# A hybrid attention and RWKV-7 layer on one core: triangular inverse issued behind the rates, unmasked and whole-run copies, projections cut into parts between the chain's links, two accumulator banks swapped

## The chip, the cores and the metric

The kernel runs on one core of one Trainium2 chip, as one launch. The metric is the time of an execution on the device in microseconds (us), lower is better. The time before is the median of three runs.

## The reference, cut to what matters

One decoder layer on x of shape (1, 512, 1024) in float32: a half-step SwiGLU network (FFN1), a mixing stage, and a second half-step SwiGLU network (FFN2). The change lies in the mixing stage alone. There one projection gives seven pieces of 512 columns; three feed a dilated attention of 8 heads, four an RWKV-7 recurrence of 8 heads of size 64.

```
proj = rms_norm(x) @ W_in                       # 1024 -> 7 x 512
q, k, v, rr, rk, rv, rc = split(proj)
att = dilated_attention(qknorm(q), qknorm(k), v)
r, k, v = lerp(rr, mu_r), lerp(rk, mu_k), lerp(rv, mu_v)   # o[t] = x[t] + (x[t-1] - x[t]) * mu
decay, a, g = small networks of rc
kk = k * k_k / norm per head
k = k * (1 + (a - 1) * k_a)
# per head, over 512 tokens:
#   S_t = S_{t-1} diag(decay_t) + (S_{t-1} (-kk_t)) (kk_t a_t)^T + v_t k_t^T ;  y_t = S_t r_t
out = (groupnorm(y) + sum(r * k * r_k) * v) * g            # the second term is called bonus here
x = x + concat(att, out) @ W_out
```

## The kernel before, in words

**Matmuls.** Large products are made from three matmuls of 128x128 by 128x512: high part by high part (line 73), low part by high part (76), high part by low part (77). A weight comes in as `raw_...` by a DMA that SyncE issues; ScalarE (ACT) rounds it to `hi_...` (line 68), VectorE (DVE) makes `lo_... = raw - hi` (line 69). One projection of 128 output columns, `proj(j, ct)`, is 24 such matmuls into a bank `in{j}_{ct}`; j is the piece (0 to 2 for q, k, v, 3 to 5 for r, k, v of the recurrence, 6 for c), ct = 0..3 the block of 128 columns, which is two heads.

**The recurrence in chunks.** The 512 tokens are cut into 8 chunks of 64. `keys1(ct)` and `keys2(ct)` prepare a block of two heads: the lerp of k, a scan of the log decays (`cs`, DVE), two exponentials (`pb`, `pi`, ACT), the normalised key. The per-head factor `hrkk` is a power on GpSimd (POOL); `spread` copies it out to 128x512 (`rbkk`, `rbk`, line 463) for four transposes on TensorE (PE). At the end of `keys2` 32 small matmuls per block write `ab{ct}{h}`, the 64x64 matrices of each chunk and head. Of each, two diagonal 32x32 quarters go into `nst` (line 547), multiplied by the mask `smask`, and one off-diagonal quarter into `nof` (line 550).

**The inverse.** `invert` inverts the 128 triangular 32x32 blocks at once: `nst` is transposed into `au`, then 31 steps, each of a product `pr` (line 582) and a subtraction into `tu` (line 584) on DVE, each pair needing the pair before it. Two transposes write `ud` and `td` (lines 588, 589). POOL copies quarters of them into `tm` and `um`. `whole(ct)` copies the diagonal blocks from `ud` into `tbd`, the matrix of whole inverses (line 608), and makes the off-diagonal ones by matmuls on PE (`w`, `u`, each with copies behind it). Only the entries of `nst` below the diagonal enter these steps.

**Rates and chain.** `rates(ct)` makes the lerps of v and r (projections 5 and 3), `rt`, and the bonus (`bo`, `bv`), whose multiplication of r is line 563. Then comes the chain of 16 links gi = 0..3 (two pairs of blocks by two halves of the sequence) by c = 0..3, one after the other, each link four heads at one chunk: PE `cx` (line 806) from the state `sv`, a DVE copy `xc`, PE `cs` with `tbd`, copies into `sv`, PE `cn` (line 823), two DVE adds into the next state (line 827), two DVE adds into `ysb` (line 829). Around the links lie `pre(gi)` (products `aa` and others), `post(gi)` (norm and gate of the output, its transposes `yo` at line 856), `qkv(ct)` (projections 0 to 2 of the attention) and the attention of (gi, c, h), in stages. A list of events `ev`, sorted by a time written out by hand, sets in which order these are issued.

**Order on the engines.** Each engine runs its instructions in a fixed order. A scheduler sets it when the kernel is built, by priorities that follow the order of the code; work under `tc.high_priority()` goes ahead of what is issued before it. A buffer is given out again when its last reader is done. The chain has two accumulator banks, "ch" (`px`, name `cx`, and `pn`, name `cn`) and "y" (`pa`, name `cs`).

```
    with tc.high_priority():
        inv = invert()
    for ct in range(NCT):
        rates(ct)
        if ct:
            whole(ct - 1, *inv)
    whole(NCT - 1, *inv)
```

Of the kernel before, what the change touches and what calls it, by code (L numbers as in the profile page):

```python
# [19 lines left out]
P = 128  # L20
# [308 lines left out]
def mixing(mc, tc, I, xT, hook, weights, mm3, proj_into, vecs, ident, nhalf, new_xT, npool, spool, dpool, set_tp, ps_c, ps_y, begin):  # L329
# [8 lines left out]
    def pm(shape, name):  # L338
        return ps_m.tile(shape, F32, tag="mm", name=name)
# [4 lines left out]
    def pc(shape, name):  # L344
        return ps_c.tile(shape, F32, tag="ch", name=name)
# [31 lines left out]
    def proj(j, ct):  # L377
        acc = pm([P, S], f"in{j}_{ct}")
        proj_into([acc], [weights(I['w_in'][j * 4 + ct], P, f"in{j}_{ct}", lo_eng=G if j == 4 else None)], xT)
        return acc  # L380


    accs = [pm([P, S], f"in6_{ct}") for ct in range(2)]
# [76 lines left out]
    def spread(r, tmp, name):  # L460

        rb = tmp([P, 8, CH], f"rb{name}")
        V.tensor_copy(out=rb, in_=r.unsqueeze(2).broadcast_to([P, 8, CH]))
        ps = pt([P, S], f"sp{name}")
        rv = rb.rearrange("p (a b) c -> p a (b c)", b=2)
        for tt in range(NT):
            T.transpose(out=ps[:, tt * P:(tt + 1) * P], in_=rv[:, tt, :], identity=ident)
        return ps
# [7 lines left out]
    def ch(t_):  # L476
        return t_.rearrange("p (c t) -> p c t", t=CH)
# [44 lines left out]
    def keys2(ct):  # L522
# [17 lines left out]
        for h in range(2):  # L540
            p_ = half(h)
            ps = pt([P, NCH, CH], f"ab{ct}{h}")
            for c in range(NCH):
                T.matmul(ps[p_, c, :], ch(bt)[p_, c, :], ch(at)[p_, c, :], start=True, stop=True)
            for b in range(2):
                q_, t_ = slice(64 * h + 32 * b, 64 * h + 32 * b + 32), slice(32 * b, 32 * b + 32)
                V.tensor_tensor(out=nstv[q_, 8 * ct:8 * ct + 8, :], in0=ps[q_, :, t_],
                                in1=smask[q_, t_].unsqueeze(1).broadcast_to([32, NCH, 32]), op=ALU.mult)
            for e in range(2):
                A.copy(out=noff[quad(h, e), :, quad(h, 1 - e)], in_=ps[quad(h, 0), e::2, 32:64])  # L550
# [22 lines left out]
    def invert():  # L573
# [13 lines left out]
        td = npool.tile([P, 32, 32], F32, tag="gain", bufs=1, name="td")  # L587
        V.transpose(out=ud.rearrange("p a b -> p (a b)"), in_=tu.rearrange("p a b -> p (a b)"))
        V.transpose(out=td.rearrange("p a b -> p (a b)"), in_=tu.rearrange("p t j -> p j t"))

        uv, tv = (z.rearrange("p t (c m e) -> p c m e t", m=4, e=2) for z in (ud, td))
        um, tm = (tmp([P, NCT, 4, 32], n) for n in ("um", "tm"))
        for h in range(2):
            for e in range(2):
                G.tensor_copy(out=tm[quad(h, e)], in_=tv[quad(h, 0), :, :, e])
                G.tensor_copy(out=um[quad(h, 1 - e)], in_=uv[quad(h, 1), :, :, e])
        return ud.rearrange("p t (a j b c) -> p a b j c t", a=2, j=2, b=2), um, tm

# [3 lines left out]
    def whole(ct, udv, um, tm):  # L602

        cp, j = ct // 2, ct % 2
        for hf in range(2):
            for q in range(4):
                q_ = slice(32 * q, 32 * q + 32)
                (V.tensor_copy if q % 2 else A.copy)(out=tbd[q_, 2 * cp + hf, j, :, q_], in_=udv[q_, cp, hf, j])
        w = tmp([P, 4, P], f"w{ct}")
# [17 lines left out]
    def qkv(ct):  # L627
        tq = lambda shape, name: gp.tile(shape, F32, tag="tq", bufs=2, name=name)
        at = lambda shape, n, t=F32R: gp.tile(shape, t, tag=f"at{n}", bufs=2, name=f"{n}{ct}")
        acc = proj(0, ct)  # L630
        sq = tq([P, S], f"sqq{ct}")
# [8 lines left out]
        G.tensor_scalar(out=nq, in0=rq, scalar1=-1.0, scalar2=0.0, op0=ALU.mult, op1=ALU.add)  # L640
        acc = proj(1, ct)
        sq = tq([P, S], f"sqk{ct}")
# [3 lines left out]
        hr = head_scale(sq, 1.0 / 64, EPS, ALU.mult, ALU.add, f"k{ct}")  # L646
        acc = proj(2, ct)
        v0 = tq([P, S], f"v0{ct}")
# [9 lines left out]
        for h in range(2):  # L658
            A.copy(out=kh[half(h), h, :], in_=kT[half(h)])
            Q.dma_start(out=kh[half(1 - h), h, :].bitcast(F32), in_=kh[half(h), h, :].bitcast(F32))  # L660
            G.tensor_tensor(out=kl[half(h), h, :], in0=kT[half(h)], in1=kh[half(h), h, :].bitcast(F32), op=ALU.subtract)
        return (qs, kh, kl), va, nq

# [73 lines left out]
    def flush():  # L737
        while any(pipe):
            attention()
# [55 lines left out]
    def chain(gi, c):  # L795
# [14 lines left out]
        if not last:  # L810
            sp = spool.tile([P, 2, CH], F32, tag="sp", bufs=2, name=f"sp{nm}")
            for h in range(2):
                V.tensor_tensor(out=sp[half(h)], in0=sv[half(h), :, h, c, :],
                                in1=pend[cp][half(h), :, cg:cg + 1].broadcast_to([64, 2, CH]), op=ALU.mult)
        pa = ps_y.tile([P, 2, 2, CH], F32, tag="y", name=f"cs{nm}")
        for j in range(2):
# [3 lines left out]

        pn = pc([P, 2, 2, CH], f"cn{nm}")
        for j, h in jh:
# [58 lines left out]
    keys2(3)  # L881
    with tc.high_priority():
        inv = invert()
    for ct in range(NCT):
        rates(ct)
        if ct:
            whole(ct - 1, *inv)
    whole(NCT - 1, *inv)
    pstack.close()
# [16 lines left out]

    def last_qkv():
        flush()
        QKV.append(qkv(3))
        mixT.extend(new_xT("mx"))  # L910
        for z in held:
            hilo(mixT[z[0]], *z[1:])

    def link(gi, c):
        with nullcontext() if gi == 2 else tc.high_priority():
            chain(gi, c)


    ev = [(-1.0, 1, lambda: QKV.append(qkv(0))), (-0.5, 1, lambda: QKV.append(qkv(1))),
          (5.5, 1, lambda: QKV.append(qkv(2))), (9.0, 1, last_qkv)]  # L920
    ev += [(t, 2 + n, lambda gi=gi: next(pres[gi], 0)) for gi, ts in enumerate(((-2, -2), (2, 2), (5, 6), (9, 9)))
# [73 lines left out]
```

## Time and profile before

| | |
|---|---|
| median of 3 runs | 1158.1 us (1154.79, 1158.1, 1160.23) |
| the profiled execution | 1164.07 us |
| its span | 1162.3 us |
| mean granted TensorE clock | 0.974 |
| busy: PE, weight loads, DVE, ACT, POOL | 1113.7, 929.9, 512.6, 370.0, 144.2 us |
| FFN2 with the end of W_out | from about 761 us to the end |

An execution took 1.8 us more than its span, which runs from the first to the last instruction in the trace. The shares of busy time are means over stages; PE is busy for 96% of the span, so that time can be lost or won only in the stretches in which it waits, or in which the granted clock is below 1.00. All times in the rows are us from the start of the span. A row in which several instructions stand together ("x10") begins at the first and gives the sum of their times. A matmul's duration is longer than its distance to the next, since matmuls are pipelined; the distance is what it costs.

### The profile page before, as it was taken

Reading aid. Unit: us, or ns where it says so; the run is one execution under the profiler, and the core shown is the slowest. Engines: PE = TensorE matmul, PEld = TensorE weight load, DVE = VectorE, ACT = ScalarE, POOL = GpSimd, SP = SyncE. Lnnn points to the kernel's source line nnn. Section 1 sums busy time; section 2 is a strip of 40 time slices with the busy share of each in tenths; the row PEclk is TensorE's granted clock in tenths of the full one; section 3 lists DMA queues with packets and bytes.
Section 4 is the critical chain, followed back from the end, with each engine's and each line's share of the span. In section 5 each row is a group of like instructions: output and inputs, shape, how many; then the busy total and the mean of one; then the engine's idle time right before and its main releaser. Section 6 shows DMA issues by size and latency. Waiting matters only on the chain.

```text
span 1162.3 us, 13792 instructions
## 1 busy us (share of the span) xinstructions
PE 1113.7 (96%) x5512; PEld 929.9 (80%) x5512; DVE 512.6 (44%) x851; ACT 370.0 (32%) x580; POOL 144.2 (12%) x189
## 2 busy tenths in 40 slices
PE   7999999999999999659999998999999999999998
PEld 6888888888888877547888888879888888888887
DVE  5333333332324438895467657545233233332222
ACT  4322322321213454132333543234232232232120
POOL 3000000000001456032522221012000000000000
PEclk9999999999999999879899998799999999999999
DMA  5323223222323523414512210051322323322421
GB/s 184 109 96 104 91 97 103 91 100 100 96 90 141 172 64 81 129 45 123 139 58 64 91 46 19 19 181 57 107 91 94 106 91 94 106 90 94 142 92 54
DMA packets 53202, 111.88 MB, mean 96 GB/s; under 512 B 20721, under 2 KB 26097, under 8 KB 53138
## 3 DMA queue, kind: packets, MB, share of 16 engines
q1 hardware_dynamic: 53138, 111.00, 29.5%
q8 instruction: 43, 0.70, 0.3%
q14 instruction: 21, 0.17, 0.0%
HBM read 100.50 MB, written 9.44 MB: 95 GB/s over the span
## 4 chain that ended last, share of the span: by engine, by line
PE 88%; DVE 6%; issue 2%; ACT 2%; DMA 1%; POOL 1%; SPq 0%; ACTq 0%; DVEq 0%; POOLq 0%
PE gu L76 14%; PE gu L77 14%; PE gu L73 14%; PE accd L76 7%; PE accd L73 7%; PE accd L77 7%; PE in L77 3%; PE in L73 3%; PE in L76 3%; PE cx L806 2%; PE aa L780 1%; PE cn L823 1%; PE acco L73 1%; PE acco L77 1%; PE acco L76 1%
## 5 line engine op out<-in xcount | busy, mean ns | idle before, releaser
L68 ACT CAST hi_gu<-raw_gu 128x1024 fp32r<-128x1024 f32 x88 | 92.9, 1055 | 315.6 <-PE gu L76 303.5
L69 DVE TENSOR_TENSOR lo_gu<-raw_gu,hi_gu 128x1024 fp32r<-128x1024 f32 x84 | 102.9, 1225 | 158.3 <-ACT hi_gu L68 154.3
L76 PE MATMUL accd<-lo_d,hh 128*128 128x512 f32 x288 | 112.3, 390 | 0.0
L77 PE MATMUL accd<-hi_d,hl 128*128 128x512 f32 x288 | 112.1, 389 | 0.0
L73 PE MATMUL accd<-hi_d,hh 128*128 128x512 f32 x288 | 112.0, 390 | 0.0
L69 DVE TENSOR_TENSOR lo_d<-raw_d,hi_d 128x1024 fp32r<-128x1024 f32 x44 | 53.3, 1224 | 128.0 <-ACT hi_d L68 127.6
L68 ACT CAST hi_d<-raw_d 128x1024 fp32r<-128x1024 f32 x44 | 45.7, 1054 | 152.2 <-PE accd L77 132.0
L198 DVE TENSOR_TENSOR sg<-gu,sg 128x512 f32<-128x512 f32 x44 | 30.4, 692 | 143.4 <-PE gu L77 142.0
L76 PE MATMUL gu<-xa0l,hi_gu 128*128 128x512 f32 (+1 forms) x184 | 70.6, 384 | 0.3 <-DVE xa0l L130 0.3
L73 PE MATMUL gu<-xa0h,hi_gu 128*128 128x512 f32 (+1 forms) x184 | 70.7, 384 | 0.0
L77 PE MATMUL gu<-xa0h,lo_gu 128*128 128x512 f32 (+1 forms) x184 | 70.4, 383 | 0.0
L73 PE MATMUL gu<-xa1h,hi_gu 128*128 128x512 f32 (+1 forms) x184 | 70.2, 382 | 0.0
L76 PE MATMUL gu<-xa1l,hi_gu 128*128 128x512 f32 (+1 forms) x184 | 70.1, 381 | 0.0
L77 PE MATMUL gu<-xa1h,lo_gu 128*128 128x512 f32 (+1 forms) x184 | 70.0, 380 | 0.0
L73 PE MATMUL gu<-xc0h,hi_gu 128*128 128x512 f32 (+1 forms) x184 | 70.0, 380 | 0.0
L73 PE MATMUL gu<-xc1h,hi_gu 128*128 128x512 f32 (+1 forms) x184 | 70.0, 380 | 0.0
L76 PE MATMUL gu<-xc0l,hi_gu 128*128 128x512 f32 (+1 forms) x184 | 69.9, 380 | 0.0
L77 PE MATMUL gu<-xc0h,lo_gu 128*128 128x512 f32 (+1 forms) x184 | 69.9, 380 | 0.0
L76 PE MATMUL gu<-xc1l,hi_gu 128*128 128x512 f32 (+1 forms) x184 | 69.9, 380 | 0.0
L77 PE MATMUL gu<-xc1h,lo_gu 128*128 128x512 f32 (+1 forms) x184 | 69.9, 380 | 0.0
L73 PE MATMUL in<-xb0h,hi_in 128*128 128x512 f32 (+1 forms) x120 | 49.7, 414 | 14.6 <-DVE r L474 9.2
L76 PEld LDWEIGHTS accd<-lo_d,hh 128*128 128x128 f32 x288 | 54.1, 188 | 11.7 <-DVE lo_d L69 0.5
(350 smaller groups left out, 2286.1 us busy)
## 6 DMA issues: line engine op xcount, KB each, us to landing
raw_gu<-in_ffn_w_gu SPq DMA_DIRECT2D x88, 512.0 KB, 3.4
raw_d<-in_ffn_w_down SPq DMA_DIRECT2D x44, 512.0 KB, 3.4
raw_in<-in_w_in SPq DMA_DIRECT2D x28, 512.0 KB, 3.5
raw_o<-in_w_out SPq DMA_DIRECT2D x8, 512.0 KB, 3.6
x<-in_x SPq DMA_DIRECT2D x4, 512.0 KB, 7.0
xd<-x SPq DMA_DIRECT2D x4, 512.0 KB, 2.6
xr<-ard SPq DMA_DIRECT2D x8, 256.0 KB, 4.4
bk<-bkd SPq DMA_DIRECT2D x4, 512.0 KB, 5.1
```

The lines of the kernel that those rows point to most:

```text
L68: A.copy(out=hi, in_=raw)
L69: (lo_eng or V).tensor_tensor(out=lo, in0=raw, in1=hi.bitcast(F32), op=ALU.subtract)
L73: first = T.matmul(ps, lh, rh, start=start, stop=False)
L76: T.matmul(ps, lh, rl, start=False, stop=False)
L77: T.matmul(ps, ll, rh, start=False, stop=stop)
L198: V.tensor_tensor(out=sg, in0=ps[1], in1=sg, op=ALU.mult)
L780: T.matmul(ps[:, c], bk[:, j, c], xr[:, j, c, 2 * h:2 * h + 2], start=True, stop=True)
L806: T.matmul(px[:, j, h], xr[:, j, c, 2 * h:2 * h + 2].rearrange("p a b -> p (a b)"), sv[:, j, h, c, :], start=True, stop=True)
L823: T.matmul(pn[:, j, h], kr[:, j, c, 2 * h:2 * h + 2].rearrange("p a b -> p (a b)"), sv[:, j, h, c, :], start=True, stop=True)
```

## The change

1. The diagonal quarters of `ab` go into `nst` by plain copies on ACT, without the mask.
2. `spread`'s copy (`rbkk`, `rbk`) moves from DVE to ACT.
3. `invert` loses its high priority and is issued after all four `rates`; the four `whole` come behind it.
4. The transposes into `ud` and `td` write with a stride, so that a block's data lies in one run; the diagonal copies into `tbd` become 16 on ACT (32x256) in place of 16 on DVE and 16 on ACT (32x128).
5. `qkv` becomes a generator: each of its projections in two halves of 12 matmuls (`proj_parts`), six steps for each ct, set into `ev` one by one. qkv(2) begins at time 4.0 (5.5 before), qkv(3) at 7.8 (9.0 before, behind a `flush` of the attention); making the mixing stage's operand tiles (`mix`) becomes an event of its own at 11.0.
6. The banks of `cs` and `cn` are swapped: `pa` goes to "ch", `pn` to "y". The next link's `cx` then takes its bank from `cs`, and not from `cn`, which the two adds into `ysb` read.

```diff
+    def proj_parts(j, ct):
+        acc = pm([P, S], f"in{j}_{ct}")
+        wh, wl = weights(I['w_in'][j * 4 + ct], P, f"in{j}_{ct}")
+        for k in range(KD):
+            if k == KD // 2:
+                yield
+            xh, xl = xT[k // 4]
+            mm3(acc, wh[:, k, :], wl[:, k, :], xh[:, k % 4, :], xl[:, k % 4, :], k == 0, k == KD - 1)
+        return acc
...
     def spread(r, tmp, name):
-        V.tensor_copy(out=rb, in_=r.unsqueeze(2).broadcast_to([P, 8, CH]))
+        A.copy(out=rb, in_=r.unsqueeze(2).broadcast_to([P, 8, CH]))
...
             for b in range(2):
-                q_, t_ = slice(64 * h + 32 * b, 64 * h + 32 * b + 32), slice(32 * b, 32 * b + 32)
-                V.tensor_tensor(out=nstv[q_, 8 * ct:8 * ct + 8, :], in0=ps[q_, :, t_],
-                                in1=smask[q_, t_].unsqueeze(1).broadcast_to([32, NCH, 32]), op=ALU.mult)
+                A.copy(out=nstv[quad(h, b), 8 * ct:8 * ct + 8, :], in_=ps[quad(h, b), :, 32 * b:32 * b + 32])
...
-        V.transpose(out=ud.rearrange("p a b -> p (a b)"), in_=tu.rearrange("p a b -> p (a b)"))
-        V.transpose(out=td.rearrange("p a b -> p (a b)"), in_=tu.rearrange("p t j -> p j t"))
+        V.transpose(out=ud.rearrange("p u t -> p t u"), in_=tu)
+        V.transpose(out=td.rearrange("p u j -> p j u"), in_=tu.rearrange("p t j -> p j t"))
...
-        for hf in range(2):
-            for q in range(4):
-                q_ = slice(32 * q, 32 * q + 32)
-                (V.tensor_copy if q % 2 else A.copy)(out=tbd[q_, 2 * cp + hf, j, :, q_], in_=udv[q_, cp, hf, j])
+        for q in range(4):
+            q_ = slice(32 * q, 32 * q + 32)
+            A.copy(out=tbd[q_, 2 * cp:2 * cp + 2, j, :, q_], in_=udv[q_, ct])
...
     def qkv(ct):
-        acc = proj(0, ct)
+        acc = yield from proj_parts(0, ct)
...
-        pa = ps_y.tile([P, 2, 2, CH], F32, tag="y", name=f"cs{nm}")
+        pa = pc([P, 2, 2, CH], f"cs{nm}")
...
-        pn = pc([P, 2, 2, CH], f"cn{nm}")
+        pn = ps_y.tile([P, 2, 2, CH], F32, tag="y", name=f"cn{nm}")
...
-    with tc.high_priority():
-        inv = invert()
     for ct in range(NCT):
         rates(ct)
-        if ct:
-            whole(ct - 1, *inv)
-    whole(NCT - 1, *inv)
+    inv = invert()
+    for ct in range(NCT):
+        whole(ct, *inv)
...
-    def last_qkv():
-        flush()
-        QKV.append(qkv(3))
+    def mix():
         mixT.extend(new_xT("mx"))
         for z in held:
             hilo(mixT[z[0]], *z[1:])
...
-    ev = [(-1.0, 1, lambda: QKV.append(qkv(0))), (-0.5, 1, lambda: QKV.append(qkv(1))),
-          (5.5, 1, lambda: QKV.append(qkv(2))), (9.0, 1, last_qkv)]
+    parts = [qkv(ct) for ct in range(4)]
+    ev = [(t, 1, lambda ct=ct: next(parts[ct], 0)) for ct, t0, dt in ((0, -1.0, 0.05), (1, -0.5, 0.05), (2, 4.0, 0.6), (3, 7.8, 0.6))
+          for t in (t0 + dt * n for n in range(6))]
+    ev += [(11.0, 1, mix)]
```

What this does to the order on three engines is shown below. A row is the line, the operation, the tile written and those read, and the shape written; the numbers in the names tell tiles apart, and the changed kernel's lines stand 10 or 11 further down.

ACT at the keys of the last block. Before, `hi_in3_1` (a weight) and the activations `sq3`, `s3` and `a3` of block 3 stood ahead of the copies from block 1's `ab10` and `ab11`:

```order
L68 CAST hi_in3_1_3538<-raw_in3_1_3536 128x1024
L493 ACTIVATE sq3_3247<-k3_3213,vec_74 128x512
L500 ACTIVATE s3_3262<-z3_3258,h0_2576 128x512
L501 ACTIVATE a3_3263<-a3_3259,h0_2576 128x512
L550 COPY nof1_3185<-ab10_3187 32x4x32 x2
L550 COPY nof1_3185<-ab11_3200 32x4x32 x2
```

and now:

```order
L68 CAST hi_in3_1_3456<-raw_in3_1_3454 128x1024
L484 ACTIVATE k3_3213<-in4_3_3214,dv_2571 128x512
L558 COPY nst_2856<-ab10_3187 32x8x32 x2
L560 COPY nof1_3185<-ab10_3187 32x4x32 x2
L558 COPY nst_2856<-ab11_3200 32x8x32 x2
L560 COPY nof1_3185<-ab11_3200 32x4x32 x2
L504 ACTIVATE sq3_3247<-k3_3213,vec_74 128x512
L511 ACTIVATE s3_3262<-z3_3258,h0_2576 128x512
L512 ACTIVATE a3_3263<-a3_3259,h0_2576 128x512
```

The four copies into `nst` and four into `nof` now stand ahead of block 3's activations. On POOL the power `hrkk3` likewise moves from behind to ahead of the step on `s3` (line 502, now 513), from which the scan starts.

DVE from the end of the inverse on. Before, it ran without a break, and the rates' work came behind it:

```order
L584 TENSOR_TENSOR tu_3375<-tu_3375,pr_3377 128x31
L588 STREAM_TRANSPOSE ud_3442<-tu_3375 128x1024
L589 STREAM_TRANSPOSE td_3443<-tu_3375 128x1024
L608 COPY tbd_2857<-ud_3442 32x4x32 x10
L474 SCALAR_TENSOR_TENSOR r0_3456<-in3_0_3457,vec_74,r0_3456 128x511
L608 COPY tbd_2857<-ud_3442 32x4x32 x6
L69 TENSOR_TENSOR lo_in0_0_3966<-raw_in0_0_3963,hi_in0_0_3965 128x1024
L563 SCALAR_TENSOR_TENSOR r0_3456<-r0_3456,vec_74,t10_2946 128x512
```

Now r0's two steps stand ahead of `au`, those of r2 behind step 11, and the low parts of the rates' last weights behind steps 20, 21 and 29 of the 31; this is the piece about steps 10, 11 and 19 to 21:

```order
L594 TENSOR_TENSOR tu_3687<-tu_3687,pr_3689 128x22x10
L485 SCALAR_TENSOR_TENSOR r2_3530<-in3_2_3531,vec_74,r2_3530 128x511
L592 TENSOR_TENSOR pr_3689<-au_3686,tu_3687 128x21x11
L594 TENSOR_TENSOR tu_3687<-tu_3687,pr_3689 128x21x11
L573 SCALAR_TENSOR_TENSOR r2_3530<-r2_3530,vec_74,t12_3160 128x512
...
L594 TENSOR_TENSOR tu_3687<-tu_3687,pr_3689 128x12x20
L69 TENSOR_TENSOR lo_in5_2_3574<-raw_in5_2_3571,hi_in5_2_3573 128x1024
L592 TENSOR_TENSOR pr_3689<-au_3686,tu_3687 128x11x21
L594 TENSOR_TENSOR tu_3687<-tu_3687,pr_3689 128x11x21
L69 TENSOR_TENSOR lo_in3_3_3613<-raw_in3_3_3610,hi_in3_3_3612 128x1024
```

The rates' steps on DVE moved from behind the inverse to places inside it; only those of block 3 remain behind `td`. On SyncE the weights' transfers `raw_in5_2`, `raw_in3_3` and `raw_in5_3` stood ahead of the transfer of `rt0`, and stand directly behind that of `rt2` now.

PE at a late link (gi = 3, c = 1). Before, transposes and products of the attention and of `post` stood between `cx111` and `cs111`:

```order
L704 MATMUL po30_5672<-va3_5271,pw300_5646 128x65
L806 MATMUL cx111_5613<-sv11_5308,xr1_3885 128x64 x4
L856 MATMUL yo10_5593<-ident_72,ysb_3898 128x128 x4
L868 MATMUL gg10_5607<-sg_2848,g2_2605 128x256
L817 MATMUL cs111_5623<-xc111_5618,tbd_2857 128x128 x2
```

and now:

```order
L817 MATMUL cx111_5597<-sv11_5171,xr1_3869 128x64 x4
L828 MATMUL cs111_5607<-xc111_5602,tbd_2857 128x128 x2
L723 MATMUL oT22_5549<-ident_72,o22_5547 128x128
L691 MATMUL sc310_5621<-kh3_5128,qs3_5127 128x256
L692 MATMUL sc310_5621<-kl1_3871,qs3_5127 128x256
L834 MATMUL cn111_5612<-sv11_5171,kr11_5181 128x64
```

`cs111` now stands directly behind `cx111`, and what filled the place stands further back. (Names: `cx` with the pair of blocks, the half and c.) The projections' last matmul stood between `cx101` and `cx102`, and stands just ahead of `cx103` now.

## Rows read from the trace of the kernel before

**Rows 1.** Busy time by stretch; last three columns: granted clock, DMA share, GB/s.

```profile
476.00:530.00 54.00, 32.27 (x109) 24.01 (x108) 47.06 (x91) 16.38 (x28) 11.34 (x11) 0.78 0.24 79
...
690.00:761.00 71.00, 63.07 (x383) 56.82 (x383) 46.63 (x137) 27.32 (x60) 11.25 (x12) 0.83 0.14 49
```

**Rows 2.** PE's waits, 476 to 560: awaited instruction; total, times, longest.

```profile
PE in L73 <- DVE r L474: 9.2, 1, 9.2
PE in L77 <- DVE lo_in L69: 6.5, 1, 6.5
```

**Rows 3.** DVE's timeline behind the inverse: start, duration.

```profile
506.70 2.04 DVE L589 STREAM_TRANSPOSE td<-tu 128x1024 f32<-128x1024 f32 x1
508.78 9.24 DVE L608 COPY tbd<-ud 32x128 f32<-32x128 f32 x10
518.05 0.75 DVE L474 SCALAR_TENSOR_TENSOR r<-in,vec,r 128x511 f32<-128x511 f32 x1
518.83 2.62 DVE L608 COPY tbd<-ud 32x128 f32<-32x128 f32 x6
```

**Rows 4.** PE's timeline: neighbours in two places.

```profile
486.39 0.63 PE L73 MATMUL in<-xb0h,hi_in 128*128 128x512 f32 x1
486.81 0.63 PE L76 MATMUL in<-xb0l,hi_in 128*128 128x512 f32 x1
...
497.61 0.39 PE L77 MATMUL in<-xb1h,lo_in 128*128 128x512 f32 x1
497.83 0.39 PE L73 MATMUL in<-xb1h,hi_in 128*128 128x512 f32 x1
```

**Rows 5.** PE's waits, 560 to 761.

```profile
PE cx L806 <- DVE ysb L829: 6.3, 7, 1.7
PE cn L823 <- ACT sv L818: 1.9, 5, 0.5
```

**Rows 6.** DVE's and POOL's groups in the keys, 430 to 476: count, busy us, mean ns.

```profile
L547 DVE TENSOR_TENSOR nst<-ab,cst 32x256 f32<-32x256 f32 x16 | 9.9, 622 | 2.2 <-PE ab L544 1.9
...
L463 DVE COPY rbkk<-hrkk 128x512 f32<-128x512 f32 x4 | 3.2, 812 | 0.0
...
L457 POOL TENSOR_TENSOR hrkk<-hmkk,nhalf 128x8 f32<-128x8 f32 x3 | 6.3, 2091 | 5.3 <-DVE hmkk L455 5.3
```

**Rows 7.** ACT's copies by form, 430 to 560.

```profile
L608 ACT COPY tbd<-ud 32x128 f32<-32x128 f32 x16 | 6.6, 410 | 6.2 <-DVE ud L588 6.0
L550 ACT COPY nof<-ab 32x128 f32<-32x128 f32 x16 | 4.1, 257 | 13.4 <-DVE nst L547 11.7 <-POOL pb L507 0.8 <-PE spkk L467 0.8
...
L772 ACT COPY sv<-vt 64x256 f32<-64x256 f32 x2 | 0.7, 372 | 0.0
```

**Rows 8.** DVE's groups, 474 to 508.8.

```profile
L582 DVE TENSOR_TENSOR pr<-au,tu 128x31 f32<-128x31 f32 (+15 forms) x31 | 10.6, 343 | 1.0
L69 DVE TENSOR_TENSOR lo_in<-raw_in,hi_in 128x1024 fp32r<-128x1024 f32 x4 | 4.9, 1220 | 1.3 <-ACT hi_in L68 1.3
...
L588 DVE STREAM_TRANSPOSE ud<-tu 128x1024 f32<-128x1024 f32 x1 | 1.2, 1246 | 0.0
```

**Rows 9.** POOL's rt, 500 to 560; a weight's transfer, 480 to 520, its last number us to landing.

```profile
L560 POOL TENSOR_TENSOR rt<-r,pb 128x512 f32<-128x512 f32 x4 | 4.8, 1193 | 15.6 <-DVE r L474 12.0 <-PE w L613 3.6
...
raw_in<-in_w_in SPq DMA_DIRECT2D x4, 512.0 KB, 3.5
```

**Rows 10.** Timeline around one link's end.

```profile
725.70 0.61 DVE L827 TENSOR_TENSOR sv<-cn,sp 64x128 f32<-64x128 f32 x2 [0.45 <-PE cn L823]
...
726.85 0.59 DVE L829 TENSOR_TENSOR ysb<-cn,xc 64x128 f32<-64x128 f32 x2
...
727.58 0.85 PE L806 MATMUL cx<-sv,xr 128*128 128x64 f32 x6 [1.03 <-DVE ysb L829]
```

**Rows 11.** The last link's `ysb` on DVE, and PE's last `yo`.

```profile
742.74 0.59 DVE L829 TENSOR_TENSOR ysb<-cn,xc 64x128 f32<-64x128 f32 x2 [0.80 <-PE cn L823]
...
751.84 0.61 PE L856 MATMUL yo<-ident,ysb 128*128 128x128 f32 x4
```

More of the change, by code (lines that the diff above doesn't have):

```diff
@@ L587, in invert @@
         td = npool.tile([P, 32, 32], F32, tag="gain", bufs=1, name="td")
-        V.transpose(out=ud.rearrange("p a b -> p (a b)"), in_=tu.rearrange("p a b -> p (a b)"))
-        V.transpose(out=td.rearrange("p a b -> p (a b)"), in_=tu.rearrange("p t j -> p j t"))
-        uv, tv = (z.rearrange("p t (c m e) -> p c m e t", m=4, e=2) for z in (ud, td))
+        V.transpose(out=ud.rearrange("p u t -> p t u"), in_=tu)
+        V.transpose(out=td.rearrange("p u j -> p j u"), in_=tu.rearrange("p t j -> p j t"))
+        uv, tv = (z.rearrange("p (c m e) t -> p c m e t", m=4, e=2) for z in (ud, td))
         um, tm = (tmp([P, NCT, 4, 32], n) for n in ("um", "tm"))
@@ L596, in invert @@
                 G.tensor_copy(out=um[quad(h, 1 - e)], in_=uv[quad(h, 1), :, :, e])
-        return ud.rearrange("p t (a j b c) -> p a b j c t", a=2, j=2, b=2), um, tm
+        return ud.rearrange("p (a b c) t -> p a b c t", a=NCT, b=2), um, tm
     tbd = mp.tile([P, 4, 2, 4, P], F32, name="tbd")
@@ L640, in qkv @@
         G.tensor_scalar(out=nq, in0=rq, scalar1=-1.0, scalar2=0.0, op0=ALU.mult, op1=ALU.add)
-        acc = proj(1, ct)
+        yield
+        acc = yield from proj_parts(1, ct)
         sq = tq([P, S], f"sqk{ct}")
@@ L646, in qkv @@
         hr = head_scale(sq, 1.0 / 64, EPS, ALU.mult, ALU.add, f"k{ct}")
-        acc = proj(2, ct)
+        yield
+        acc = yield from proj_parts(2, ct)
         v0 = tq([P, S], f"v0{ct}")
@@ L661, in qkv @@
             G.tensor_tensor(out=kl[half(h), h, :], in0=kT[half(h)], in1=kh[half(h), h, :].bitcast(F32), op=ALU.subtract)
-        return (qs, kh, kl), va, nq
+        QKV.append(((qs, kh, kl), va, nq))
     mixT, held = [], []
```

## The prediction

> **What bounds the kernel now.** I read the page's table of slices first: PE is busy almost everywhere, and its clock falls below full in two places of the mixing stage. So the change, which leaves both SwiGLU networks alone, can pay only where PE waits or where its clock is low. Busy time by stretch then gives two such places [rows 1]. From 476 to 530 us PE is busy for 32.27 of 54 us, so it waits 21.7 us, at a granted clock of 0.78. From 690 to 761 us it waits 7.9 of 71 us, at 0.83: 0.17 x 71 = 12.1 us of clock are not granted, some 24 us at the lower of the two levels (1.2 of 2.4 GHz). What a matmul costs at each level is seen between neighbours: 0.42 us at half, 0.22 us at full [rows 4].
>
> PE's waits say what ends them. In the first place two are large: 9.2 us for the lerp of r and 6.5 us for a low part [rows 2]. DVE's timeline shows why: behind the inverse ten copies into `tbd` take 9.24 us, and only then, at 518.05, comes r0's lerp [rows 3]. So PE stands because the inverse and its copies go ahead of the rates on DVE. In the second place it is the chain: `cx` waits for `ysb` 6.3 us in 7 waits [rows 5], because `cx` needs the bank that the `ysb` adds still read.
>
> **The change part by part.** PE's matmuls stay the same, so I sum what changes in its waits and in its time at half clock.
>
> *Keys (up to the inverse's start).* DVE loses 16 masked copies of 0.62 us and four of `rbkk` of 0.81 us, 13.2 us in all [rows 6]; ACT gains both. Four of the copies into `nst` and four into `nof` now stand ahead of block 3's activations on ACT, and the power `hrkk3`, 2.09 us [rows 6], ahead of the step from which its scan starts on POOL. The trace has no such copy on ACT. From below, a copy of as many elements takes 0.37 us. From above, copies of half as many take 0.41 us with a strided side and 0.26 without, so 0.37 + 2 x 0.15 = 0.67 [rows 7]. I take 0.5, an estimate between them. Four are 2.0 us, four copies into `nof` 1.0, about 3 us on the way to block 3's scan; the power may hide behind them. DVE, freed of its part, gives some 1.2 us of it back before `ab` of block 3. So **+1.8 us** (0 to +3.5, with the dearer copies and the power in full). `au` then starts at about 475.8 in place of 474.1.
>
> The Trainium skill, page "SBUF — State Buffer", section "Specifications (TRN2)", says that each access that crosses to a new 16-byte line pays a penalty, which speaks against copies that write with a stride. The trace agrees as far as it goes, 410 against 257 ns [rows 7]; by the rule the four copies would be 0.7 us dearer together than I take them, and the sum that much higher.
>
> *Inverse and rates.* The 9.2 us go, since r0 now stands ahead of `au`. But the inverse itself is not shorter: 62 steps, of which the 31 products take 343 ns each and the 31 subtractions as much [rows 8], about 23 us with the gaps. The rates' lerps and bonuses (0.75 us each [rows 3]) and low parts (1.22 us [rows 8]) now stand between these steps, and PE waits for them in turn. I walked both lists. PE has 42 projection matmuls and two bonuses behind `ab`, ready at 484.6, and waits 0.8 us for the second bonus's r1. On DVE `au` ends at 477.1, ten steps take 7.3 us, r1's lerp and product, v1's and r2's lerps and two bonuses among them 4.3, step 11 0.85, r2's product 0.75: 490.3. PE waits 4.9 us for it. The weights of blocks 2 and 3 are now issued behind `rt2`, on SP. r2's lerp ends at 488.7, `rt2` takes 1.2, the transfer 3.5 [rows 9], the cast about 1: `hi_in5_2` is there at 494.5, and PE waits 3.8 us. `lo_in5_2` stands behind step 20, 499.6: 4.5 us more. Then 1.3 us for the last bonus's r3 (`td` ends at 515.8, 7 us later than before), 2.0 us for the first `w`, 3.6 us for the `u` steps and the first `aa`. Together 20.9 us of waits against 21.7: **-0.8 us**. They are shorter ones, though. In the trace half clock shows behind the long waits, as at 486.39 behind the 6.5 us [rows 2, 4]; I count three such stretches with 5.5 us lost before, and take half to stay: **-2.8 us**. Bounds for the two: if `lo_in5_2` and `rt2` come 3 us later than walked, +3; if the full clock holds and the `u` steps lie under the projections, -8.
>
> The `tbd` copies now lie on ACT and behind nothing. DVE wins 11.9 us by it [rows 3], but behind the inverse, where PE already has the attention's first projections to do. The transposes write with a stride: the one that reads so took 2.04 us against 1.25 [rows 3, 8]; I count 0.8 us for each, in the 515.8 above.
>
> The same page, section "Who interferes with whom", says that DVE and GpSimd share a pair of ports, and that whichever starts first locks the other out; a DVE operation with two inputs counts. The trace agrees: the ten copies that ran beside POOL's copies took 0.92 us each, the six behind them 0.44 [rows 3]. By this rule `lo_in0_0` and r3 would wait for POOL's copies now, and the last bonus come 1 to 2 us later.
>
> *Bank swap.* In the late link DVE ends the new `sv` at 726.31, and PE's `cx` starts at 727.58, after the `ysb` adds that end at 727.44 [rows 10]. With `cs` in the bank that `cx` takes, this wait is gone at every link; `cn` now waits for the `ysb` of the link before, which is long done. Not all of the 6.3 us [rows 5] is won: `cs` now stands directly behind `cx` in the late links, so PE meets the wait for `xc` or for the copies into `sv`, like the 1.9 us that `cn` waits already [rows 5]. I take **-4.5 us** (-6.3 to 0).
>
> *Projections in halves.* The same 288 matmuls lie nearer the links. The last now stands ahead of `cx103`, about 0.7 of a link later than before, so PE has filling longer, and 12.1 us of clock to win back [rows 1]. The last links have none. I take a good quarter: **-3.5 us** (-8 to 0). At the end `post` stands behind low parts of W_out and `pw` on DVE; the last `yo` came 9.1 us after the last `ysb` [rows 11], and one low part more puts it 1.2 us later: **+1.3 us** (0 to +3).
>
> Sum: 1.8 - 0.8 - 2.8 - 4.5 - 3.5 + 1.3 = -8.5 us. The profiled execution took 1164.07 us (1162.3 of span and 1.8 around it), so 1155.6. The runs' median is 6 us lower, 1158.1; with the same sum it gives **1149.6**, or 0.7% less.
>
> **Rivals.** A run of this kernel can't tell less than 0.5% (5.8 us) from no change: 1152.3 to 1163.9 is the same.
>
> *The clock holds in the late links.* Waits of a microsecond before each `cx` are what precedes half clock there (727.58 [rows 10]). Without them what matmuls lose to it there, by the distances of neighbours about 9.7 of the 12.1 us, could come back: 6 us more, **1143.5**. Against it: five links without projections.
>
> *The waits only change their name.* `cx` no longer waits, but `cs` waits for `xc` and `cn` for `sv`, and the projections held open take one of four banks from the attention, so that scores wait for them. Then the swap gives 1.5 and the clock nothing: 1.8 - 0.8 - 2.8 - 1.5 + 1.3 = -2.0, **1156**, the same. For it: those waits stand in the list already [rows 5], and a chain of dependent steps isn't shortened by filling placed elsewhere.
>
> *Slower: half clock over the late links.* With `cs` straight behind `cx` PE pauses twice in each link, and nothing of the projections fills the last five. If PE stays at half clock there, each us of it costs about 0.47 us (0.42 against 0.22 a matmul [rows 4]). To end 5.8 us above the median, my clock term must be +11 and not -3.5: 23 us more at half, so 47 us of the 71 in place of 24. From there on the change loses; at 50 us it gives about **1165**. For it: the two places of low clock are the two with waits [rows 1]. Against it: those waits were longer than these would be.
>
> *Nothing changes* can't be: the order differs on every engine.
>
> **How the numbers follow.** My forecast, 0.36. The clock holds, 0.22. Waits renamed, 0.26. Slower, 0.16. So the forecast is 1149.6. The first two cases lie below 1152.3, the third within, the fourth above, and a part of the forecast's own bounds (a keys stretch of +3.5 and rates of +3) reaches into the same: faster 0.57, same 0.28, slower 0.15. The range goes from 1139 (the clock held and the inverse at its lower bound) to 1162 (past the renamed waits, short of half clock); some 1 in 10 lies on either side. The forecast's own range is 1144 to 1155.
>
> **What would show it.** `au` starts at 474 to 478, and `td` ends near 516. PE's list has no wait for r over 6 us and none for `ysb`. `tbd` copies stand on ACT at 0.4 to 0.7 us. The granted clock from `aa` to the first `acco` with `mx1h` is above 0.93, and in the last 71 us of mixing above 0.85. Wrong it would be if `au` started after 480, if the waits for `xc` and `sv` came to over 5 us together, or if the clock of the late links stayed under 0.8.

## The result and the profile after

The changed kernel takes 1144.24 us, the median of 8 runs (1142.18 to 1151.76). The kernel before took 1159.16 us in the same series (8 runs, 1154.14 to 1165.42). The ratio is 0.9869, with an interval of 0.9843 to 0.9896: 1.3% faster, where the prediction said 0.7%. The time lies in the range given, at the lower end of the forecast's own 1144 to 1155, and next to the first rival's 1143.5.

Its profiled execution took 1145.14 us with a span of 1143.4 us. First the windows of both kernels, cut at the same places of the program: from 430 us to the first product `aa`, from there to 70 us before the first matmul of W_out with `mx1h`, and those 70 us. Columns as in [rows 1]; before:

```profile
430.00:559.90 129.90, 103.95 (x555) 82.10 (x554) 101.21 (x177) 45.11 (x90) 43.96 (x58) 0.91 0.38 103
559.90:690.90 131.00, 125.71 (x808) 109.22 (x808) 78.25 (x214) 53.32 (x106) 38.04 (x41) 0.96 0.23 70
690.90:760.90 70.00, 62.07 (x375) 55.82 (x374) 45.63 (x134) 26.32 (x58) 11.25 (x12) 0.83 0.14 49
```

and after:

```profile
430.00:553.40 123.40, 103.79 (x544) 81.14 (x543) 79.78 (x141) 56.97 (x110) 41.59 (x58) 0.90 0.41 113
553.40:670.50 117.10, 112.23 (x746) 98.59 (x745) 72.78 (x197) 48.73 (x98) 35.64 (x39) 0.99 0.23 71
670.50:740.50 70.00, 65.80 (x448) 58.54 (x447) 51.00 (x147) 33.33 (x70) 14.04 (x14) 0.98 0.16 57
```

PE's waits are a window's length less PE's busy time. Up to the first `aa` they fell from 25.95 to 19.61 us, in the two later windows together from 13.22 to 9.07: 10.5 us. PE's busy time fell by 9.9 us (291.73 to 281.82) with the same matmuls, which is for the most part half clock avoided; the last window rose from 0.83 to 0.98. Mixing ends 20.4 us earlier, and the second SwiGLU network with the rest of W_out took 402.9 us in place of 401.4, so that the spans differ by 18.9.

PE's waits up to the first `aa`, from 476 us, columns as in [rows 2]:

```profile
PE bo L577 <- DVE r L573: 6.5, 3, 4.2
PE in L73 <- ACT hi_in L68: 4.8, 1, 4.8
PE in L77 <- DVE lo_in L69: 1.9, 1, 1.9
```

These are 13.2 us, where the same view of the kernel before sums to 21.7, 9.2 of them in one wait [rows 2]. From the first `aa` to the end of mixing, the view of [rows 5] now begins:

```profile
PE cs L828 <- DVE xc L820: 1.7, 3, 0.6
PE yo L867 <- DVE ysb L862: 1.3, 1, 1.3
PE spk L478 <- ACT rbk L474: 1.2, 1, 1.2
PE cn L834 <- DVE sv L830: 0.9, 2, 0.6
```

No `cx` waits for the adds into `ysb` any more. A late link shows it, where [rows 10] had the wait:

```profile
708.78 0.61 DVE L838 TENSOR_TENSOR sv<-cn,sp 64x128 f32<-64x128 f32 x2
...
709.21 1.12 PE L817 MATMUL cx<-sv,xr 128*128 128x64 f32 x8
...
709.94 0.29 DVE L840 TENSOR_TENSOR ysb<-cn,xc 64x128 f32<-64x128 f32 x1
...
710.84 0.71 PE L828 MATMUL cs<-xc,tbd 128*128 128x128 f32 x4 [0.52 <-DVE xc L820]
```

`cx` starts inside the add into `sv`, and ahead of `ysb`; what PE waits for now is `xc`, 0.52 us.

Runs of one kernel differ by more than these waits, and the mean granted clock of each run goes with its time: the changed kernel's 1142.18 us came at 0.987, its 1151.76 at 0.978; the kernel before ran between 0.973 and 0.986. A least-squares fit over the 210 executions whose clock is on record, of all the kernels here, with one offset for each kernel and one slope for all, gives 0.77 us for each 0.001 of mean clock, with a scatter of 1.2 us. So each result below has two columns more: its median clock, and the fit's time at a clock of 0.985 against the kernel before's there (1155.9 us). I read the second as what waits and order are worth, and the rest as clock. The rest is not mere noise: an edit can move the clock that most runs of its kernel are granted, as e5 and e12 show below. The fit is good to about 1 us, and the runs come from four chips, on which the kernel before differs by up to 1.3 us at one clock.

| kernel | median us | ratio to before, interval | clock | at 0.985 |
|---|---|---|---|---|
| before, all series | 1159.1 | | 0.980 | 0 |
| changed | 1144.2 | 0.9869, 0.9843 to 0.9896 | 0.9875 | -9.7 |
| e1, swap alone | 1163.1 | 1.0020, 1.0002 to 1.0037 | 0.975 | -0.3 |
| e2, halves alone | 1157.8 | 0.9984, 0.9967 to 1.0001 | 0.9785 | -4.5 |
| e8, swap and halves | 1161.3 | 1.0001, 0.9977 to 1.0025 | 0.974 | -2.6 |
| e3, all up to the chain | 1157.1 | 0.9968, 0.9945 to 0.9991 | 0.980 | -2.6 |
| e6, inverse's place alone | 1155.3 | 0.9975, 0.9947 to 1.0002 | 0.9825 | -3.3 |
| e4, changed less swap | 1152.9 | 0.9936, 0.9913 to 0.9959 | 0.982 | -4.8 |
| e9, changed less halves | 1152.2 | 0.9941, 0.9915 to 0.9966 | 0.981 | -6.6 |
| e5, changed less ACT copies | 1155.1 | 0.9939, 0.9912 to 0.9966 | 0.975 | -9.0 |
| e10, before with filling | 1160.3 | 1.0006, 0.9988 to 1.0024 | 0.985 | +4.4 |
| e12, e5 with filling | 1145.8 | 0.9880, 0.9847 to 0.9913 | 0.988 | -7.9 |
| e11, changed, weights first | 1141.7 | 0.9848, 0.9816 to 0.9881 | 0.988 | -11.9 |
| e13, e12 with weights first | 1142.5 | 0.9847, 0.9818 to 0.9876 | 0.9885 | -11.6 |

The changed kernel's 14.9 us are thus some 9.7 us of waits and order, and 5.8 us (7.5 times 0.77) of clock. The profiled execution before had a clock of 0.974, at the low end of its runs, and so the two traces show more clock won than the medians do: at 0.77 us the difference to the median's 0.980 is 4.6 us.

### The profile page after: what moved, and what is told of

The parts are those of the page before. It is cut to its first block, busy times and chain, and to the rows that moved or that the text cites. A ratio compares the mean times of both kernels' runs of the same rounds, so it can differ in the third digit from the quotient of the medians.

```text
span 1143.4 us, 13773 instructions
## 1 busy us (share of the span) xinstructions
PE 1103.1 (96%) x5512; PEld 919.7 (80%) x5512; DVE 491.1 (43%) x811; ACT 383.9 (34%) x604; POOL 142.1 (12%) x189
## 5 line engine op out<-in xcount | busy, mean ns | idle before, releaser
L76 PEld LDWEIGHTS accd<-lo_d,hh 128*128 128x128 f32 x288 | 54.1, 188 | 11.6 <-DVE lo_d L69 0.5
L77 PEld LDWEIGHTS accd<-hi_d,hl 128*128 128x128 f32 x288 | 54.1, 188 | 11.3
```

The costliest lines, as they stand in the source:

```text
L76: T.matmul(ps, lh, rl, start=False, stop=False)
L77: T.matmul(ps, ll, rh, start=False, stop=stop)
```

## The experiments

The theory at the outset: the bank swap removes waits in the links, and with them the half clock there. The rivals: the halves keep the clock up; the earlier stage gives the gain; the waits only change their names.

**e1, the swap alone**, in the kernel before:

```diff
-        pa = ps_y.tile([P, 2, 2, CH], F32, tag="y", name=f"cs{nm}")
+        pa = pc([P, 2, 2, CH], f"cs{nm}")
-        pn = pc([P, 2, 2, CH], f"cn{nm}")
+        pn = ps_y.tile([P, 2, 2, CH], F32, tag="y", name=f"cn{nm}")
```

> The kernel before with the two chain banks swapped and nothing else. If the swap alone gives the chain's gain (waits and clock): about -10 us, ratio near 0.991, no wait for ysb, and the granted clock from 690 us to the end of mixing above 0.93. If the swap only takes its waits away and the clock comes from the projections' new places: -3 to -5 us, ratio near 0.997, clock there still about 0.83. If the waits only change their names: -1.5 us, ratio near 0.999, with waits for xc and sv of 4 us or more.

Ratio 1.0020, slower if anything. The theory falls. From the first `aa` to the end of mixing PE's waits in e1 are headed by:

```profile
PE cs L817 <- DVE xc L809: 2.4, 5, 0.7
PE cx L806 <- DVE sv L827: 1.7, 2, 1.5
PE cn L823 <- ACT sv L818: 1.4, 4, 0.4
PE aa L780 <- DMA bk<-bkd: 1.3, 1, 1.3
```

The 6.3 us for `ysb` [rows 5] are gone, and the chain's next steps have 5.5 us in the first three rows, where the kernel before had 2.4 (1.9 for `sv` [rows 5] and 0.5 for `xc`). The last 70 us ran at 0.85. Alone, the swap does what the rival of the renamed waits said.

**e2, the halves alone**: `proj_parts`, `qkv` as a generator, the new times and `mix`, as in the change's diff.

> The kernel before with the projections in halves on the new times and the mix event, banks as before. If filling the links is what keeps the clock up: -8 us or more, ratio near 0.993, clock in the late links above 0.93 although the waits for ysb remain. If the swap does it: within 3 us of before, ratio 0.998 to 1.003, ysb waits of 6 us and a clock of about 0.83 remain.

Ratio 0.9984, and -4.5 us at the same clock; waits for `ysb` of 4.4 us remain, and 0.88 in the last 70 us. From the first `aa` on PE's waits in its trace are 10.3 us in place of 13.2. The halves shorten waits, and alone they do not keep the clock (0.9785 against 0.980).

**e3, all up to the chain**: copies, transposes and the inverse's place, as in the change's diff; chain and events as before.

> The kernel before with the changes up to the chain alone (copies on ACT without the mask, strided transposes, inverse behind the rates); banks and projections as before. By the two traces the stretch up to the first aa product won about 3.3 us: ratio near 0.997, with PE's waits from 430 us to that product at 18 to 21 us in place of 26. If the later links take the gain back, or lose more clock: ratio 0.999 to 1.002.

Ratio 0.9968, as expected; waits up to the first `aa` were 19.7 us. At the same clock e3 is worth 2.6 us, less than the 6.3 us of waits won there: from the first `aa` on its trace has 15.2 us of waits in place of 13.2. Its profiled execution, at 0.986 near the top of its runs (0.976 to 0.987), had full clock in the last 70 us, though PE still waited there for `ysb` ahead of `cx`, up to 1.5 us at a time (window, then wait):

```profile
678.10:748.10 70.00, 61.64 (x424) 53.39 (x423) 51.16 (x141) 32.50 (x68) 12.87 (x13) 1.00 0.17 56
```

```profile
PE cx L804 <- DVE ysb L827: 3.3, 4, 1.5
```

**e4, the changed kernel without the swap** (e1's diff read backwards).

> The changed kernel with the two banks put back. If the swap gives the chain's gain: +8 to +12 us against the changed kernel, ratio to before near 0.996, waits for ysb of 5 us or more, clock in the late links about 0.85. If the swap gives its waits alone: +4 us, ratio near 0.990, clock still above 0.93. If it gives nothing: ratio near 0.987.

Ratio 0.9936: here the swap is worth 4.9 us at the same clock, and 8.6 us in the median. The waits for `ysb` that come back are 1.4 us only, and the last 70 us ran at 0.85. What is worth nothing alone is worth 5 us when the rest stands: the next two runs ask with what.

**e8, swap and halves** in the kernel before, and **e9, the changed kernel without the halves**, that is, the earlier stage and the swap:

> The kernel before with the banks swapped and the projections in halves, nothing else. Alone the swap measured 1.002 and the halves 0.998. If the two work only together (the swap takes the wait away, the halves fill the links then): ratio near 0.992, -9 us. If the swap needs the earlier stage's order instead: ratio 0.999 to 1.001, the sum of the two.

> The changed kernel with the projections whole and at the old times (swap and early stage kept). If swap and halves need each other: ratio near 0.998, the early stage's 0.997 with the swap's 1.002. If swap and early stage need each other: ratio near 0.990, close to the changed kernel. The half-clock loss in the late links should follow the same split.

e8 measured 1.0001 (-2.6 us at the same clock, less than the halves alone), e9 0.9941 (-6.6). So by the times at one clock the swap's partner is the earlier stage: e9 is 4.0 us below e3, and e8 1.9 above e2. That the clock follows the same split did not hold: e9 had 0.981, like the kernel before, and so its ratio lies halfway between the two expected. By the table, then, the halves are worth 3.1 us on top of the other two (e9 against the changed kernel), the swap 4.9 and the earlier stage 7.1 (e8), and among these runs the clock of 0.9875 comes only with all three.

**e5, the changed kernel with the copies back on DVE**:

```diff
-        A.copy(out=rb, in_=r.unsqueeze(2).broadcast_to([P, 8, CH]))
+        V.tensor_copy(out=rb, in_=r.unsqueeze(2).broadcast_to([P, 8, CH]))
...
-                A.copy(out=nstv[quad(h, b), 8 * ct:8 * ct + 8, :], in_=ps[quad(h, b), :, 32 * b:32 * b + 32])
+                V.tensor_tensor(out=nstv[q_, 8 * ct:8 * ct + 8, :], in0=ps[q_, :, t_],
+                                in1=smask[q_, t_].unsqueeze(1).broadcast_to([32, NCH, 32]), op=ALU.mult)
```

> The changed kernel with the masked products into nst and spread's copy back on DVE (inverse placement, strided transposes, halves and swap kept). If the copies on ACT are what puts the inverse's start 8 us later at 482.9: au starts near 475, PE's waits in the keys fall by 2 to 3 us, and the time is 1 to 4 us below the changed kernel, ratio near 0.985. If DVE's relief is worth more than ACT's load: au no earlier, 2 to 5 us slower, ratio 0.989 to 0.991.

`au` starts at 474.6 in place of 482.9, as the first reading had it, and the keys' waits fall. Yet the median is 10.9 us above the changed kernel's, the clock 0.975, and at the same clock the two are alike (-9.0 and -9.7). The waits from 476 us to the first `aa` show why an inverse that starts 8 us earlier wins nothing:

```profile
PE in L73 <- ACT hi_in L68: 6.7, 1, 6.7
PE bo L578 <- DVE r L574: 6.4, 2, 3.5
PE in L77 <- DVE lo_in L69: 5.4, 1, 5.4
```

18.5 us in place of 13.2: the same weights are late, and PE comes to them sooner. The median, though, is no accident of a few runs: 9 of e5's 12 had a clock of 0.976 or less, and three had 0.984 or more and took 1144.7 to 1149.3 us, while of the changed kernel's 8 runs one had 0.978, at 1151.8 us.

**e10, filling**, in the kernel before: four more matmuls (eight instructions on PE) behind `cn` in links of gi = 2 and 3, into a part of the bank that nobody reads.

```diff
+            pnx = pc([P, 2, 4, CH], f"cn{nm}")
+            pn = pnx[:, 0].rearrange("p (a b) c -> p a b c", a=2)
...
+        if gi >= 2:
+            for _ in range(4):
+                T.matmul(pnx[:, 1, 0:2].rearrange("p a c -> p (a c)"), ident, ident, start=True, stop=True)
```

> The kernel before with four more 128x128 matmuls behind cn in the last eight links, into a part of the bank that nobody reads: about 1.1 us of work in each, where PE otherwise waits up to 1.7 us for ysb. If pauses of PE before each cx cause the half clock there: the granted clock of the last 70 us of mixing rises above 0.93, and the time falls by 2 to 6 us in spite of the work, ratio 0.995 to 0.998. If the clock has another cause: still 0.76 to 0.87, and the time grows by 0 to 5 us, ratio 1.000 to 1.004.

The clock rose as the first theory says: all 12 runs lie at 0.983 or more, where the kernel before has a median of 0.980. The time stayed (1.0006): the filling cost 4.4 us at the same clock, and the clock gave about as much back (5 times 0.77).

**e12, the same filling in e5**:

> The changed kernel with the copies back on DVE, whose runs mostly had a mean clock of 0.975 (1155.1 us), and four more 128x128 matmuls behind cn in the last eight links, as in the other run with such filling. If the late links lose their clock because PE does too little there: mean clock 0.983 or more in most runs, the last 70 us of mixing near 1.00, and 1148 to 1153 us, ratio 0.990 to 0.994. If the clock falls there for another reason: 0.975 as before, and 1156 to 1162 us, ratio 0.997 to 1.002.

1145.8 us in place of 1155.1, below the range expected, by 32 matmuls whose result nobody uses; at the same clock they cost 1.1 us; all 6 runs lie at 0.985 or more. The last 70 us of mixing of e5, then of e12, then of e10:

```profile
679.10:749.10 70.00, 65.53 (x353) 57.69 (x352) 43.74 (x122) 28.06 (x60) 11.64 (x11) 0.78 0.17 57
```

```profile
673.30:743.30 70.00, 66.88 (x468) 60.31 (x467) 48.06 (x140) 32.04 (x66) 12.41 (x13) 0.98 0.16 56
```

```profile
685.90:755.90 70.00, 62.39 (x454) 55.54 (x454) 47.05 (x138) 28.79 (x62) 12.18 (x12) 1.00 0.15 48
```

e5 waits 4.5 us there, 0.4 of it ahead of `cx`, and runs at 0.78; e10 waits 7.6 us, 0.6 of it ahead of `cx`, and e3, without filling, 8.4 us, 3.3 of it ahead of `cx`, and both run at 1.00. So waits ahead of `cx` do not bring half clock by themselves, and half clock comes without them. More work for PE in the links raised the clock in both kernels. It did not do so by moving the projections: five links stand behind their last matmul in e5 and in e12, six in the kernel before and in e10. But the order of other work on PE in the links differs too in both pairs, so that the added work is the likely cause, and not shown to be the only one.

**e6, the inverse's place alone**, in the kernel before:

```diff
-    with tc.high_priority():
-        inv = invert()
     for ct in range(NCT):
         rates(ct)
-        if ct:
-            whole(ct - 1, *inv)
-    whole(NCT - 1, *inv)
+    inv = invert()
+    for ct in range(NCT):
+        whole(ct, *inv)
```

> The kernel before with the inverse issued behind the rates at ordinary priority, and all else as before. If this move is what wins in the stretch up to the first aa product: au stays near 474, PE waits 19 to 22 us there in place of 26, ratio near 0.997, as all the early changes together. If it needs the cheaper copies into tbd and on ACT: waits of 25 us or more, ratio 0.999 to 1.002.

Ratio 0.9975, with an interval that just reaches 1, and -3.3 us at the same clock, like e3 with the copies and transposes added. The waits up to the first `aa` are 24.1 us, so neither expectation was met whole: the place seems to carry the early gain, but only 1.8 us of it are fewer waits in that stretch; PE's busy time there is 1.9 us less.

**e11, the rates' weights first**, in the changed kernel:

```diff
-        Q.dma_start(out=raw, in_=src)
+        with tc.high_priority() if name[:3] in ("in3", "in5") else nullcontext():
+            Q.dma_start(out=raw, in_=src)
```

> The changed kernel with the transfers of the rates' weights (projections 3 and 5) issued at high priority on SP, so that those of blocks 2 and 3 no longer stand behind rt2's; nothing else is edited. If that queue makes PE's waits for hi_in5_2 and lo_in5_2 (4.8 and 1.9 us in the changed kernel): both are gone, PE waits 11 to 14 us up to the first aa product in place of 19.6, 4 to 7 us faster than the changed kernel at the same mean clock, ratio near 0.982. If the wait moves to the next link of DVE's chain (r2, v2, the inverse itself): within 2 us of the changed kernel, ratio 0.986 to 0.989, with the same sum of waits under other names.

1141.7 us, 2.2 us below the changed kernel at the same clock; the medians' intervals overlap. The waits from 484 us to the first `aa`:

```profile
PE w L623 <- POOL tm L606: 4.9, 1, 4.9
PE in L74 <- ACT kts L656: 2.8, 1, 2.8
PE u L630 <- DVE w L627: 1.7, 2, 1.5
PE in L78 <- DVE lo_in L70: 1.1, 1, 1.1
```

The 4.8 us for `hi_in5_2` is gone, and 4.9 us for the inverse's end (`tm`) stands in its place: the second theory, nearly. From 430 us on the waits are 17.8 us in place of 19.6. The edit moved more than the weights: the first `aa` comes at 561.4 us, 8 us later than in the changed kernel, with 36 matmuls more ahead of it.

**e13, e12 with e11's edit**, so that the inverse starts early and the weights too:

> The changed kernel with three edits of earlier runs together: the rates' weights first on SP, the copies into nst and of spread back on DVE, and the filling of the last eight links. With the weights behind rt2, an inverse that starts 8 us earlier was worth nothing at the same mean clock. If that was because PE then waits for the weights instead: now the wait of w for tm (4.9 us in the run with the weights first) falls below 2 us, and the time is 1136 to 1140 us, ratio 0.980 to 0.983, at a mean clock of 0.985 or more. If the inverse's start is never what PE waits for: 1141 to 1144 us, ratio 0.984 to 0.987, with the filling's price of about 1 us.

1142.5 us, as the second theory has it: `w` waits 2.7 us for `tm` now, and a weight's `hi_in` 4.9 us again. It does not beat e11, though two of its six runs took 1137.0 and 1137.2 us, at a clock of 0.992.

## Why the prediction was right, and where it was off

**The sign and the bound** held: the gain lies in mixing alone, in the two places read from [rows 1]. That the time came to lie beside the first rival's 1143.5 is luck: the rival sums to 12.3 us of clock and 2.2 of waits, and the table has 5.8 and 9.7. By the prediction's own 0.47 us for each us at half, the 24 us of [rows 1] also cost 11.3 us and not the 9.7 that this rival counts.

**Keys, +1.8 us.** PE's waits up to the inverse's start grew by 2.6 us (3.8 of 44.1 before, 6.4 of 52.9 after). A copy into `nst` took 0.605 us on ACT, inside the bounds 0.37 to 0.67 and nearer the upper one. But `au` started at 482.9, not at 475.8: the trace of after shows the copies, then block 3's activations, then the power, not hidden as I thought it might be.

```profile
457.88 1.21 ACT L558 COPY nst<-ab 32x256 f32<-32x256 f32 x2
459.11 0.53 ACT L560 COPY nof<-ab 32x128 f32<-32x128 f32 x2
459.66 0.72 ACT L504 ACTIVATE sq<-k,vec 128x512 f32<-128x512 f32 x1
...
462.27 1.64 POOL L468 TENSOR_TENSOR hrkk<-hmkk,nhalf 128x8 f32<-128x8 f32 x1 [7.47 <-DVE hmkk L466]
463.88 0.62 POOL L513 TENSOR_SCALAR s<-s 128x512 f32<-128x512 f32 x1
...
464.54 1.66 DVE L516 TENSOR_TENSOR_SCAN cs<-scanm,s 128x512 f32<-128x512 f32 x1 [2.35 <-POOL s L513]
```

What the term put at nothing is clock. The stretches up to `au` and from there to the first `aa`, before:

```profile
430.00:474.10 44.10, 40.30 (x283) 32.75 (x282) 36.10 (x51) 16.66 (x33) 22.11 (x27) 1.00 0.39 87
474.10:559.90 85.80, 63.64 (x273) 49.36 (x272) 65.11 (x127) 28.45 (x57) 21.85 (x31) 0.86 0.37 111
```

and after:

```profile
430.00:482.90 52.90, 46.50 (x286) 36.54 (x285) 27.66 (x34) 30.24 (x56) 23.22 (x28) 0.90 0.36 83
482.90:553.40 70.50, 57.29 (x259) 44.60 (x259) 52.12 (x108) 26.72 (x55) 18.37 (x30) 0.90 0.46 134
```

PE is busy 6.2 us longer in the keys with three matmuls more, and half clock stands behind a wait for block 3's `sq`, where neighbours lie 0.42 us apart:

```profile
460.43 1.56 PE L464 MATMUL hskk<-cst,sq 128*128 128x2 f32 x8 [1.78 <-ACT sq L504]
...
462.85 0.63 PE L73 MATMUL in<-xb0h,hi_in 128*128 128x512 f32 x1
463.27 0.63 PE L76 MATMUL in<-xb0l,hi_in 128*128 128x512 f32 x1
```

The copies on ACT go with it: from 446 us to `au` the clock is 0.91 to 0.95 in all five traces of kernels that have them there (changed, e3, e4, e9, e11), and from 446 to 473.6 us it is 1.00 in the nine others. By the prediction's own sign `au` past 480 would make it wrong. The sum survived, since PE had the rates' projections to do meanwhile; e5, with `au` at 474.6, is no faster at the same clock. The other signs held, but for `td`, which ended at 522.7 us and not near 516.

**Inverse and rates, -0.8 us of waits: the step that failed.** The walk gave 20.9 us of waits; 13.2 came. Its single waits were 0.8, 4.9, 3.8, 4.5 and 1.3 us, and 5.6 for `w`, the `u` steps and `aa`. Measured were 0.91, 4.16, 4.76, 1.90 and 1.48, and nothing for the last. There PE is busy throughout (windows view, after):

```profile
535.00:553.00 18.00, 18.00 (x108) 15.38 (x108) 9.25 (x22) 9.02 (x24) 5.84 (x14) 1.00 0.64 176
```

I charged the `u` steps as before, although the order already put the attention's projections between them. With the keys the waits up to the first `aa` are 6.3 us fewer, where the sum said 1.0 more. The queue on SP was rightly found: `rt2`'s transfer, then the weights, then PE.

```profile
496.57 1.26 SPq L572 DMA_DIRECT2D ard<-rt  x2
497.93 1.54 SPq L64 DMA_DIRECT2D raw_in<-in_w_in  x3
...
502.47 1.04 ACT L68 CAST hi_in<-raw_in 128x1024 fp32r<-128x1024 f32 x1 [8.38 <-DMA raw_in<-in_w_in]
...
503.57 0.79 PE L73 MATMUL in<-xb0h,hi_in 128*128 128x512 f32 x1 [4.76 <-ACT hi_in L68]
```

The half clock of this stretch, -2.8 us by the sum, did fall: 14% of 85.8 us were not granted before and 10% of 70.5 are now, 12.0 us against 7.1, which is about 10 us less at half, or 4.7 us by the prediction's 0.47. But the keys lost as much: none of 44.1 us before, 10% of 52.9 now.

**Transposes.** `ud` took 2.11 us, 0.86 more than [rows 8], as counted; `td`, which reads and writes with a stride, took 2.15 and not 2.8.

**Bank swap, -4.5, and the end, +1.3.** Waits from the first `aa` on fell by 4.15 us, where the two terms say 3.2. The size is right; the reason was incomplete. The swap removes its wait alone too, but its gain comes only with the earlier stage's order: -0.3 us alone, 4.9 us on top of the rest (e4). That 4.9 is near the 4.5 of the sum is therefore in part luck. Why that order and the swap need each other was not settled: the scheduler places other work in each of these kernels.

**Clock, -2.8 and -3.5 us.** Together -6.3, and the medians show -5.8. But by the traces the early stretches gave nothing together, and it came all in the links. The two terms were read from an execution at 0.974 and charged to a median at 0.980, which has 4.6 us less clock to win. The rival of the held clock was right on what happens there: 7 of the changed kernel's 8 runs lie at 0.986 to 0.989. Its reason, that waits before `cx` bring half clock, does not hold (e5 and e3). The third rival's, that the pauses behind `cx` do it, fares no better: the changed kernel waits 1.0 us for `xc` in the last 70 us, e5 1.4, at 0.98 and 0.78. The filling shows that added work on PE goes with a higher clock there. Why e4, e5 and e9, each one part short of the change, mostly lose the clock there and the changed kernel mostly keeps it was not settled; no run here varies the links' work in steps.

**Halves, in waits: a term put at nothing.** The sum charged the halves with clock alone, -3.5 us. Alone they gave no clock, and 4.5 us at the same clock (e2); on top of the rest they are worth 3.1 us at the same clock (e9) and clock besides.

So the size, 1.3% in place of 0.7%, was missed in the waits: waits and order are worth 9.7 us at the same clock, and the four terms on them summed to 2.2. By the two traces most of this lies ahead of the first `aa`, where PE's waits came out 7.3 us below the sum (6.3 fewer and not 1.0 more); from there on they are 1.0 us below it. The early stage alone has the same waits there (e3), but is worth 2.6 us only, since PE waits longer in the links behind it; the gain is whole only with swap and halves beside it. Why the three gain more together than alone stays open.

## What to carry to other kernels

Compare runs at the same granted clock before giving a difference to an edit: here 0.010 of mean clock is 8 us, as much as most edits are worth, and an edit that is worth under 1 us at the same clock (the copies on ACT) moved the median by 10.9 us, because it moved the clock of most runs. So give both numbers. When a wait is charged again in the new order, look up what the order now puts between its two ends; an engine that has other work there does not wait. Two terms can sum to the right number and both be wrong, as those on the clock did here, so check each in its own stretch. A part that measures as nothing alone can be worth 5 us beside another, so leave-one-out runs are needed as well as one-alone runs.

## What was unexpected of the hardware

Work for nothing made the kernel faster: 32 matmuls of 128x128 took e5 from 1155.1 to 1145.8 us, by a mean clock of 0.988 in place of 0.975.

A step of the inverse stands still when GpSimd works beside it. In the trace of after:

```profile
495.29 1.26 POOL L570 TENSOR_TENSOR rt<-r,pb 128x512 f32<-128x512 f32 x1 [8.52 <-DVE r L485]
...
495.12 0.39 DVE L592 TENSOR_TENSOR pr<-au,tu 128x231 f32<-128x231 f32 x1
495.55 1.25 DVE L594 TENSOR_TENSOR tu<-tu,pr 128x231 f32<-128x231 f32 x1
```

The subtraction, 0.40 us at its other occurrence with this shape, takes 1.25 and ends at 496.80, just after `rt` at 496.55. The Trainium skill, page "SBUF — State Buffer", section "Who interferes with whom", has this as a DVE operation with two inputs that meets a GpSimd operation reading SBUF; the trace agrees, also in that the one that starts later waits. The 16 copies into `tbd` on ACT took 403 ns for 32x256, no more than the 410 ns for half as many with a strided source [rows 7].
